# A decoder trunk with three attention branches: a new driver for the order of scores, outputs and projections

## The chip, the cores and the metric

The kernel runs on one core of a Trainium2 chip. The metric is the device time of one execution in microseconds (us), median of several runs.

## What is computed

One layer (sequence 2048, width 1024): a normalised input is projected once, and three causal token mixers of width 512 read their queries, keys, values and a gate path z from it. Their outputs, times SiLU of z, are projected, gated per channel by a sigmoid, summed and sent through the output projection. The inputs and outputs are float32.

```python
proj = rmsnorm(x, norm_g) @ w_in              # q, k, v, z of three branches, fox_f, merge gates
# differential: 4 heads of 2 score maps; ALiBi bias
pd = softmax(s[0]) - lam * softmax(s[1]);  oa = rmsnorm(pd @ v) 
# forgetting: 8 heads; bias c[q] - c[k], c the cumulative log_sigmoid of fox_f
ob = softmax(q @ k.T * scale + c_q - c_k) @ v
# dilated: 8 heads; windows of 128 steps at strides 1, 4 and 16, merged by their row maxima
y = stack([oa, ob, oc]) * silu(z)
merged = sum(sigmoid(merge_g) * (y @ w_branch), axis=branch)
out = rmsnorm(x + merged @ w_out, final_g)
```

## The kernel before

Every float32 operand is split into a high and a low float16 part, and a projection is three products (high by high, high by low, low by high) accumulated in one PSUM bank. After a start-up that normalises and transposes x and projects the first queries and keys, twelve groups are run (g 0 to 11): four differential, four forgetting and four dilated ones, each with the heads that fill 128 channels. A merge and an output projection close the kernel.

A group has two kinds of work on TensorE. The **fill** is projections: generators (`fill_v`, `proj_unit` of the next group, `fill_z`, `fill_gate`) in the queue of the class `Filler`, whose `step` runs the head of the queue for one step of six matmuls of 512 columns, counted at 216 ns each; `pump(ns)` runs steps until a credit of ns is used, and moves chains of side work (the finish of the group before, weight preparation) along. One projection of 128 channels over all tokens is TP = 4 x 24 x 216 ns = 20.736 us. The **attention** is written as jobs of 128 queries (two or four blocks in the dilated groups). A job has a generator S (scores) and a generator T (transposes):

- S: for each chunk of up to 512 keys two matmuls into one of three score banks (`scores`), then VectorE adds the bias and takes the row maximum into a float32 weight tile (L678, L1049; five such tiles, `E_SLOTS`). At the end ScalarE takes the exponential (L691, L1055); in the differential groups VectorE then combines the two maps (L784).
- T: ScalarE and VectorE split the weights into float16 parts in place (L702, L703), and SyncE issues a DMA transpose (L712) into one of three transposed tiles (`ET_SLOTS`). A generator for the output matmuls (`pv_mm`, L695 and L696) goes into the list `pvq`.

In the old `drive`, scores run up to three jobs ahead of the job that is transposed, as long as fewer than the allowed weight tiles are live; 0.2 of a job's share of the fill (`SFRAC`) is pumped between its chunks, the rest around its transposes and outputs. Outputs are run as soon as more than two (`LAG`) are in the list. The share of a job goes by a cost (differential: n(2 x 2 x 56 + 165) + 1500 for n key blocks), and the total is multiplied by 1.1 (`XF`).

What is written in this order is a priority. The framework's scheduler runs its own timing model over the program, and hands each engine, whenever the model has it free, the ready instruction that was written first. An instruction that is not ready in the model lets later ones pass; on the chip each engine then runs its list in order.

The functions that the diff touches, with the line numbers of the profile:

Of the kernel before, what the change touches and what calls it, by code (L numbers as in the profile page):

```python
# [19 lines left out]
P = 128  # L20
# [4 lines left out]
HD = 64  # L25
# [12 lines left out]

E_SLOTS = 5
V_SLOTS = 4  # L40
LAG = 2
SFRAC = 0.2
CHAIN = 1.3
XF = 1.1
XT = 1.1
PS = 1.5
WR = 1.0
W_SLOTS = 3
# [31 lines left out]
class Filler:  # L80
    def __init__(self):
        self.queue = []
        self.credit = 0.0
        self.chains = []
        self.wq = []
        self.wc = 0.0
# [18 lines left out]
    def step(self):  # L105
        while self.queue:
            c = next(self.queue[0], END)
            if c is END:
                self.queue.pop(0)
                continue  # L110
            return c
        return None

# [40 lines left out]
def tile_hybrid_trunk(  # L154
# [65 lines left out]
        V.tensor_mul(dst, dst, t)  # L220

    fl = Filler()
    sgx = ExitStack()
    xpool = sgx.enter_context(tc.tile_pool(name="xpool", bufs=1))
    xT = [[xpool.tile([P, KC, 512], F16, tag=f"xT{i}_{tg}", name=f"xT{i}_{tg}") for tg in range(4)] for i in range(2)]
# [142 lines left out]
    def mm_steps(dst, pairs, ns, per):  # L368
        n = len(pairs)
        for i, (l, r) in enumerate(pairs):  # L370
            T.matmul(dst, l, r, start=(i == 0), stop=(i == n - 1))  # L371
            if (i + 1) % per == 0 or i == n - 1:
                yield ns * per

    def mm_all(dst, pairs):
        n = len(pairs)
        for i, (l, r) in enumerate(pairs):
            T.matmul(dst, l, r, start=(i == 0), stop=(i == n - 1))

    def proj_unit(gr, j, tgs=range(4)):  # L380
        name = f"{gr['n']}_{j}"
# [258 lines left out]

    def scores(gr, u, q2s, qsl, ps, ksl):
        stk = gr["stk"][u]
        T.matmul(ps, stk[:, 0, qsl], stk[:, 1, ksl], start=True, stop=False)  # L643
        T.matmul(ps, q2s, stk[:, 1, ksl], start=False, stop=True)  # L644

    def make_q2(gr, u, i):
        stk = gr["stk"][u]
# [6 lines left out]
    def softmax_rows(gr, u, q2, qb, bias_of, diag, den_of, name):  # L654
        n = qb + 1
        nk = n * P
        nch = (n + 3) // 4
        qsl = slice(P * qb, P * qb + P)
        off = P * (qb % 4)
        pm = st1("pm", f"pm_{name}", 5)  # L660
        np_ = 0
        et = []
        for ch in range(nch):
            w = min(512, nk - 512 * ch)
            if ch % 2 == 0:
                et.append(e_tile(f"e_{name}_{ch // 2}", (P, 1280)))
                live[0] += 1
            ps = sc_bank(f"s_{name}_{ch}")
            scores(gr, u, q2[:, off:off + P], qsl, ps[:, :w], slice(512 * ch, 512 * ch + w))
            o = 256 + 512 * (ch % 2)  # L670
            segs = [(0, w, bias_of(512 * ch, w))]
            if diag is not None and ch == nch - 1:
                segs = [(w - P, P, diag)]
                if w > P:
                    segs.append((0, w - P, bias_of(512 * ch, w - P)))
            for a, sw, b in segs:
                with hp(H_TT):
# [3 lines left out]
            yield  # L681
# [12 lines left out]
    def pv_mm(po, eh, el, vv, first, last):  # L694
        T.matmul(po, eh, vv, start=first, stop=False)  # L695
        T.matmul(po[:, 0], el, vv[:, 0], start=False, stop=last)  # L696

    def split_in_place(t, c, w, scale):
        f = t[:, 256 + 512 * c:256 + 512 * c + w]
# [12 lines left out]
            Q.dma_start_transpose(eh[:, 0:2 * n // P], e[:, :n].bitcast(F16))  # L712
        return eh

    def transposed_pv(et, n, dd, vsel, scale, name, fin):
        box = {}

        def pv(i, eh):
            if i == 0:
                box["po"] = po_bank(f"po_{name}")  # L720
            po = box["po"][:, :2 * dd].rearrange("p (a c) -> p a c", a=2)
            for ch in range(2 * i, min(2 * i + 2, (n + 3) // 4)):
                nb = min(4, n - 4 * ch)
                for b in range(nb):
                    kb = 4 * ch + b
                    o = 8 * (ch % 2) + b
                    pv_mm(po, eh[:, o], eh[:, o + nb], vsel(kb), kb == 0, kb == n - 1)
# [21 lines left out]
    def jobs_diff(gr):  # L749
# [7 lines left out]
        def job(qb):  # L757
# [30 lines left out]
            def T_():  # L788
# [5 lines left out]
                yield from transposed_pv(hold["e"], n, P, lambda kb: gr["v"][kb // 4][:, kb % 4:kb % 4 + 5:4], lamA, name, fin)  # L794
# [128 lines left out]
    def jobs_fox(gr):  # L923
# [6 lines left out]
        def job(u, qb):  # L930
# [15 lines left out]
            def T_():  # L946
# [3 lines left out]
                def fin(po):  # L950
# [1 line left out]
                    A.activation(yq, po[:, 0], AF.Copy)  # L952
                    V.tensor_add(yq, yq, po[:, 1])

                yield from transposed_pv(hold["e"], n, HD, vsel, 2.0 ** 14, name, fin)

            ne = (n + 7) // 8
            nch = (n + 3) // 4
            return {"S": S_, "T": T_, "nS": nch, "nT": ne, "v": n,
                    "cost": n * (2 * 56 + 86)}  # L960

        return [job(u, qb) for u in range(2) for qb in range(NB)]

# [43 lines left out]
    def jobs_dil(gr):  # L1007
# [7 lines left out]
        def job(p, bs):  # L1015
# [11 lines left out]
            def S_():  # L1027
# [3 lines left out]
                for h in range(0, len(bs), 2):  # L1031
# [6 lines left out]
                    for a, b in enumerate(bs[h:h + 2]):  # L1038
# [17 lines left out]
                        yield  # L1056

            def T_():
                eh = transpose_tile(hold["e"], widths, 2.0 ** 14, name)

                def pv():
# [27 lines left out]
                            Q.dma_start(v, ro)  # L1089
                        yield  # L1090

                pvq.append(pv())
                yield

            return {"S": S_, "T": T_, "nS": len(bs), "nT": 1, "v": bs[-1] + 1 if p == 0 else NB,
                    "cost": sum(2 * kn[b] * (2 * 56 + 86) for b in bs)}

        return [job(p, list(range(b0, b0 + (2, 2, 4)[p]))) for p in range(3) for b0 in range(0, NB, (2, 2, 4)[p])]

# [75 lines left out]

    pvq = []

    def drive(gr, cap, limit, total_fill):
        jobs = jobmakers[gr["br"]](gr)
        n = len(jobs)  # L1180
        wts = [jb["cost"] + 1500 for jb in jobs]
        tw = sum(wts)
        sj = 0
        sgen = jobs[0]["S"]()
        for i, jb in enumerate(jobs):
            share = total_fill * wts[i] / tw
            tgen = jb["T"]()
            while True:
                while sj < n and (sj <= i or sj - i <= limit) and live[0] < cap:
                    if next(sgen, END) is not END:  # L1190
                        fl.pump(SFRAC * total_fill * wts[sj] / tw / jobs[sj]["nS"])
                    else:
                        sj += 1
                        if sj < n:
                            sgen = jobs[sj]["S"]()
                        else:
                            gr["Sdone"] = True
                assert sj > i
                while gr["vdone"] < jb["v"]:
                    c = fl.step()  # L1200
                    assert c is not None and c >= 0, (gr["n"], i)
                if next(tgen, END) is END:
                    break
                sh = (1 - SFRAC) * share / jb["nT"]
                while len(pvq) > LAG:
                    for _ in pvq.pop(0):
                        fl.pump(0.5 * sh)
                        sh *= 0.5
                fl.pump(sh)
# [250 lines left out]
    T.transpose(pb[:, :KC], g8, ident[:KC, :KC])  # L1460
    V.tensor_copy(gx, pb[:, :KC])
    gm = st.tile([P, 1], F32, tag="gm", name="gm")
    V.tensor_reduce(gm, gx, axis=AX.X, op=ALU.max, apply_absolute_value=True)
# [31 lines left out]
        w_start()  # L1495

    TP = 4 * 24 * 216
    for g in range(12):
        gr = groups[g]
        nx = groups[g + 1] if g < 11 else None  # L1500
        total = (2 + NG[g]) * TP
        fl.add(fill_v(gr))
        if g > 0:
            gr["post"] = fl.chain(post(groups[g - 1]))
        if nx is not None:
            fl.add(proj_unit(nx, 0))
            fl.add(fill_z(gr))
            total += TP
            if g == 2:
                fprep = fl.chain(prep_f())  # L1510
                fl.add(fill_f())
                total += 20000
# [4 lines left out]
        else:  # L1517
            fl.add(fill_gate((22,)))
            fl.add(tail_fill(gr))
            total = 4 * TP * XT  # L1520
# [89 lines left out]
```

## Time and profile before

| what | value |
|---|---|
| median of 3 runs | 2789.35 us (2782.4 to 2799.62) |
| profiled execution, first to last instruction | 2783.2 us |
| TensorE busy in it | 2624.6 us |
| VectorE busy | 2088.2 us |
| ScalarE busy | 1661.3 us |
| GpSimd busy | 376.8 us |

The profile is of one execution. Its own time is given as the span from its first to its last instruction; it lies 6 us below the median of the runs and inside their range. Busy shares are sums over the span and say nothing on which engine another one waits for.

### The profile page before, as it was taken

To read this page: it belongs to the slowest core of one execution; us is meant where nothing else is said; L and a number is where in the kernel's file an instruction comes from. 1 tells how busy PE (TensorE), PEld (TensorE's weight loads), DVE (VectorE), ACT (ScalarE), POOL (GpSimd) and SP (SyncE) were. 2 spreads that over 40 slices of the span, in tenths; PEclk is the share of its full clock that TensorE was granted. 3 is DMA by queue.
4 is the path that set the end of the run, shared out by engine and by line. 5 is a ranking of instruction groups with operands and counts; after the bars stand their busy time and mean duration, and the time that the engine had idled before them with its cause. 6 is when DMAs were issued, how large, how long until landed. Compare 5 with 4: busy or idle time off the path is not lost.

```text
span 2783.2 us, 47508 instructions
## 1 busy us (share of the span) xinstructions
PE 2624.6 (94%) x16216; PEld 1376.9 (49%) x16216; DVE 2088.2 (75%) x7048; ACT 1661.3 (60%) x3616; POOL 376.8 (14%) x529
## 2 busy tenths in 40 slices
PE   7999899999999999999899999999999999999998
PEld 4454445455444454444444444554554545444565
DVE  8687877978877878768778776658568575778955
ACT  6466666656556676666666665656657678535411
POOL 0000200200201112002102110005033051210000
PEclk9999999989999999999999999999999999999999
DMA  4345444445454786787787777648568599875232
GB/s 160 76 84 114 74 100 107 104 76 123 87 100 106 135 173 142 155 154 157 144 155 145 141 144 156 132 108 180 126 132 185 125 210 230 226 210 163 80 121 76
DMA packets 979268, 376.94 MB, mean 135 GB/s; under 512 B 834120, under 2 KB 939344, under 8 KB 977488
## 3 DMA queue, kind: packets, MB, share of 16 engines
q1 hardware_dynamic: 979024, 373.90, 61.9%
q8 instruction: 127, 2.08, 0.3%
q14 instruction: 117, 0.96, 0.1%
HBM read 118.14 MB, written 59.05 MB: 64 GB/s over the span
## 4 chain that ended last, share of the span: by engine, by line
PE 52%; DVE 19%; DMA 17%; ACT 7%; issue 4%; POOL 1%; SPq 1%; DVEq 0%; ACTq 0%; POOLq 0%
DMA eT_g<-e_g 11%; PE pg L371 10%; PE pbr L371 8%; PE pq_g L371 8%; PE pz_g L371 5%; PE pout L1417 4%; PE s_g L643 4%; DVE e_g L678 4%; PE s_g L644 4%; DVE e_g L703 4%; PE po_g L695 3%; ACT e_g L691 3%; PE pv_g L371 2%; PE pout L1418 2%; DMA w_g<-in_w_in_dram 2%
## 5 line engine op out<-in xcount | busy, mean ns | idle before, releaser
L371 PE MATMUL pg<-xT,w_g 128*128 128x512 f16 x2304 | 554.5, 382 | 0.3 <-ACT xT L638 0.3
L691 ACT ACTIVATE e_g<-e_g,nm_g,c_g 128x1024 f32<-128x1024 f32 (+7 forms) x384 | 377.6, 984 | 263.5 <-DVE nm_g L685 227.9
L643 PE MATMUL s_g<-stk_g 128*128 128x512 f16 (+3 forms) x1024 | 352.6, 352 | 50.2 <-DVE pm_g L678 45.6
L703 DVE SCALAR_TENSOR_TENSOR e_g<-e_g 128x512 f16<-128x512 f32 (+2 forms) x480 | 316.0, 670 | 80.9 <-ACT e_g L702 79.6
L371 PE MATMUL pq_g<-xT,w_q 128*128 128x512 f16 x1536 | 369.5, 387 | 5.0 <-DVE stk_g L398 4.4
L695 PE MATMUL po_g<-v_g,eT_g 128*128 128x128 f16 (+1 forms) x2232 | 306.7, 235 | 61.5 <-DMA eT_g<-e_g 56.2
L644 PE MATMUL s_g<-stk_g,q_g 128*128 128x512 f16 (+3 forms) x1024 | 351.9, 354 | 2.6 <-DMA q_g<-stk_g 2.6
L371 PEld LDWEIGHTS <-w_g 128*128 128x128 f16 x2304 | 218.9, 99 | 229.9 <-issue 5.3
L702 ACT ACTIVATE e_g<-e_g 128x512 f16<-128x512 f32 (+2 forms) x480 | 265.0, 569 | 104.4 <-DVE e_g L703 102.3
L696 PE MATMUL po_g<-v_g,eT_g 128*128 128x64 f16 (+1 forms) x2232 | 286.3, 201 | 0.0
L695 PEld LDWEIGHTS <-eT_g 128*128 128x128 f16 x2232 | 207.2, 99 | 141.7 <-DMA eT_g<-e_g 88.4
L371 PE MATMUL pz_g<-xT,w_z 128*128 128x512 f16 x1152 | 273.1, 380 | 2.5 <-DVE stk_g L398 2.4
L371 PE MATMUL pv_g<-xT,w_v 128*128 128x512 f16 x1152 | 270.3, 382 | 4.3 <-DVE vs_g L527 4.3
L1055 ACT ACTIVATE e_g<-e_g,nm_g,c_g 128x256 f32<-128x256 f32 (+1 forms) x384 | 207.8, 543 | 91.4 <-DVE nm_g L1051 90.3
L371 PE MATMUL pbr<-u,w_b 128*128 128x512 f16 x1152 | 253.5, 381 | 0.0
L678 DVE CUSTOM_DVE_ANT_0 e_g<-s_g,bias_g 128x512 f32<-128x512 f32 (+3 forms) x320 | 187.8, 605 | 59.7 <-DMA eT_g<-e_g 51.6
L696 PEld LDWEIGHTS <-eT_g 128*128 128x128 f16 x2232 | 204.5, 99 | 49.5 <-issue 5.5
L371 PEld LDWEIGHTS <-w_q 128*128 128x128 f16 x1536 | 146.5, 100 | 166.4 <-issue 13.4
L678 DVE CUSTOM_DVE_ANT_0 e_g<-s_g,R_g 128x512 f32<-128x512 f32 (+3 forms) x288 | 171.2, 596 | 62.9 <-DMA eT_g<-e_g 55.4
L1049 DVE CUSTOM_DVE_ANT_0 e_g<-s_g,bd_g 128x256 f32<-128x256 f32 (+1 forms) x384 | 122.8, 361 | 89.0 <-PE s_g L644 44.7
L371 PEld LDWEIGHTS <-w_b 128*128 128x128 f16 x1152 | 112.9, 98 | 133.5 <-issue 2.2
L644 PEld LDWEIGHTS <-q_g 128*128 128x128 f16 x1024 | 109.2, 107 | 140.6 <-issue 62.3
(471 smaller groups left out, 4174.3 us busy)
## 6 DMA issues: line engine op xcount, KB each, us to landing
gd<-gs SPq DMA_DIRECT2D x96, 256.0 KB, 2.7
gt<-gd SPq DMA_DIRECT2D x24, 1024.0 KB, 5.3
w_g<-in_w_in_dram SPq DMA_DIRECT2D x24, 512.0 KB, 4.4
ud<-y_g SPq DMA_DIRECT2D x48, 256.0 KB, 2.8
od_g<-ro_g SPq DMA_DIRECT2D x64, 132.0 KB, 1.9
xb<-in_x_dram SPq DMA_DIRECT2D x16, 512.0 KB, 5.8
q_g<-stk_g SPq DMA_DIRECT2D x128, 64.0 KB, 2.2
w_q<-in_w_in_dram SPq DMA_DIRECT2D x32, 256.0 KB, 4.1
```

The source lines that it names most:

```text
L371: T.matmul(dst, l, r, start=(i == 0), stop=(i == n - 1))
L643: T.matmul(ps, stk[:, 0, qsl], stk[:, 1, ksl], start=True, stop=False)
L644: T.matmul(ps, q2s, stk[:, 1, ksl], start=False, stop=True)
L678: V.tensor_tensor_reduce(out=et[ch // 2][:, o + a:o + a + sw], in0=ps[:, a:a + sw], in1=b, scale=1.0, scalar=-3e38, op0=ALU.add, op1=ALU.m ...
L691: A.activation(e[:, 256:256 + w], e[:, 256:256 + w], AF.Exp, bias=nm, scale=gr["c"][u], accum_out=den_of(i))
L695: T.matmul(po, eh, vv, start=first, stop=False)
L696: T.matmul(po[:, 0], el, vv[:, 0], start=False, stop=last)
L702: A.activation(h[:, :w], f, AF.Copy, scale=scale)
L703: V.scalar_tensor_tensor(h[:, w:], f, scale, h[:, :w], op0=ALU.mult, op1=ALU.subtract)
L1049: V.tensor_tensor_reduce(out=e[:, o + w * u:o + w * u + w], in0=ps[:, 256 * u:256 * u + w], in1=bt[p, u][:, 256 - w:256], scale=1.0, scala ...
L1055: A.activation(eu, eu, AF.Exp, bias=nm[:, 2 * a + u:2 * a + u + 1], scale=gr["c"][u], accum_out=sm[:, a, 2 + u:3 + u])
L1417: T.matmul(po, ah, wo[un][k], start=k == 0, stop=False)
```

## The change

`drive` is rewritten. Jobs are written strictly one after the other, scores and then transposes, with no run-ahead. After each chunk of w key columns the loop pumps total_fill x w / (sum of w), where w is the chunk's columns (twice two blocks in the dilated groups) plus `STEP` = 150. The factors `SFRAC`, `XF`, `XT` and `LAG` are gone, and the dilated groups pump 8 us of fill (`lead`) ahead of their first chunk.

The `Filler` gets a clock that counts what TensorE is given: each fill step by its count, each chunk by 0.84 w, each output step by 600. An output generator is entered with the time clock + `LAT` (12000 for differential, 9000 for the other groups) and is run when the clock has passed it, between fill steps too, or earlier when three are waiting and a new transpose is to be written (`pv_room`). After the last job, `drain` pumps what is left in steps of 1300 with the outputs between.

Each score and output matmul also gets a dependence in order alone (no semaphore) on the last fill matmul written before it, so that the scheduler may not move it ahead of that. It may still move fill ahead of a score or an output that is not ready. These ties hold in the twelve groups alone.

```diff
-LAG = 2
-SFRAC = 0.2
-XF = 1.1
-XT = 1.1
+LAT = (12000, 9000, 9000)
+STEP = 150
...
+            if c:
+                self.clock += max(c, 0)
             return c
...
+    def after_fill(ins):
+        if pe_last[0] is not None:
+            tc.add_manual_dep(ins.ins, pe_last[0], mybir.DependencyInfo(mybir.DependencyClass.NoSync, mybir.DependencyReason.DATA),
+                              reason="order")
+
+    def mm_fill(*a, **k):
+        ins = T.matmul(*a, **k)
+        if pe_last[0] is not None:
+            pe_last[0] = ins.ins.name
+
+    def mm(*a, **k):
+        after_fill(T.matmul(*a, **k))
...
-            T.matmul(dst, l, r, start=(i == 0), stop=(i == n - 1))
+            mm_fill(dst, l, r, start=(i == 0), stop=(i == n - 1))
...
-        T.matmul(ps, stk[:, 0, qsl], stk[:, 1, ksl], start=True, stop=False)
-        T.matmul(ps, q2s, stk[:, 1, ksl], start=False, stop=True)
+        mm(ps, stk[:, 0, qsl], stk[:, 1, ksl], start=True, stop=False)
+        mm(ps, q2s, stk[:, 1, ksl], start=False, stop=True)
...
+            pv_room()
             eh = transpose_tile(e, [512] * (w // 512) + ([w % 512] if w % 512 else []), scale, f"{name}_{i}")
-            pvq.append(pv(i, eh))
+            pv_add(pv(i, eh), gr, n)
...
-            return {"S": S_, "T": T_, "nS": 2 * nch, "nT": ne, "v": n, "cost": n * (2 * 2 * 56 + 165)}
+            return {"S": S_, "T": T_, "w": 2 * (nk + STEP * nch)}
...
+    def pv_add(gen, gr, need):
+        pvq.append((gen, fl.clock + LAT[gr["br"]], gr, need))
+
+    def pv_run():
+        gen, _, gr, need = pvq.pop(0)
+        while gr["vdone"] < need:
+            c = fl.step()
+            assert c is not None and c >= 0, gr["n"]
+        for _ in gen:
+            fl.clock += 600
+
+    def pv_room():
+        while len(pvq) >= ET_SLOTS:
+            pv_run()
+
+    def pv_due():
+        while pvq and fl.clock >= pvq[0][1]:
+            pv_run()
+
+    def pump(ns):
+        fl.pump_chains(ns * CHAIN)
+        fl.credit += ns
+        while fl.credit > 0:
+            c = fl.step()
+            if c is None or c < 0:
+                fl.credit = 0.0
+                return
+            fl.credit -= c
+            pv_due()
+
+    def drive(gr, total_fill, lead):
         jobs = jobmakers[gr["br"]](gr)
+        tw = sum(jb["w"] for jb in jobs)
+        total_fill -= lead
+        pump(lead)
+        for jb in jobs:
+            for w in jb["S"]():
+                fl.clock += 0.84 * w
+                pv_due()
+                pump(total_fill * w / tw)
+            run_all(jb["T"]())
+        gr["Sdone"] = True
+
+    def drain():
+        while fl.queue:
+            pump(1300)
         while pvq:
-            run_all(pvq.pop(0))
+            pv_run()
+        fl.drain()
...
-        total = (2 + NG[g]) * TP
+        total = (2 + NG[g]) * TP + (TP if nx is not None else 0)
...
-        drive(gr, E_SLOTS - (2 if gr["br"] == 2 else 0), 3, total * XF)
-        fl.drain()
+        drive(gr, total, 8000 if gr["br"] == 2 else 0)
+        drain()
+    pe_last[0] = None
```

## Rows read from the trace of the kernel before

**Rows 1.** The page, part 1: busy us of each engine, share, instructions.
```profile
PE 2624.6 (94%) x16216; PEld 1376.9 (49%) x16216; DVE 2088.2 (75%) x7048; ACT 1661.3 (60%) x3616; POOL 376.8 (14%) x529
```

**Rows 2.** Busy time by stretch: length, five engines, clock, DMA share, GB/s.
```profile
130.00:960.00 830.00, 784.00 (x4766) 407.59 (x4765) 673.86 (x2174) 509.89 (x1020) 89.19 (x89) 0.98 0.49 101
960.00:1680.00 720.00, 666.17 (x4736) 348.51 (x4735) 547.02 (x1910) 468.96 (x953) 104.86 (x163) 1.00 0.77 149
1680.00:2400.00 720.00, 691.89 (x4198) 368.82 (x4196) 493.99 (x1855) 477.50 (x1268) 146.05 (x222) 0.97 0.75 162
2400.00:2784.00 384.00, 373.87 (x1990) 194.78 (x1988) 277.81 (x744) 129.97 (x230) 31.95 (x45) 0.99 0.46 140
```

**Rows 3.** Timeline of TensorE, forgetting stage: start us, us, instructions of one kind merged.
```profile
1059.80 0.38 PE L644 MATMUL s_g<-stk_g,q_g 128*128 128x512 f16 x1
1060.02 4.48 PE L371 MATMUL pq_g<-xT,w_q 128*128 128x512 f16 x20
```

**Rows 4.** Waits of TensorE, 130 to 960 us: total us, times, longest.
```profile
PE s_g L643 <- DVE pm_g L678: 27.9, 44, 3.9
PE po_g L695 <- DMA eT_g<-e_g: 7.1, 11, 2.4
PE pv_g L371 <- DVE vs_g L527: 4.3, 4, 2.2
```

**Rows 5.** Waits of TensorE, 960 to 1680 us.
```profile
PE po_g L695 <- DMA eT_g<-e_g: 37.4, 33, 2.3
PE s_g L643 <- DVE pm_g L678: 11.8, 16, 1.5
```

**Rows 6.** Waits of TensorE, 1680 to 2400 us.
```profile
PE po_g L695 <- DMA eT_g<-e_g: 11.6, 11, 3.1
PE pq_g L371 <- DVE stk_g L398: 3.9, 2, 2.1
```

**Rows 7.** Timeline of TensorE, a dilated group of stride 16.
```profile
2350.33 0.43 PE L644 MATMUL s_g<-stk_g,q_g 128*128 128x128 f16 x1
2350.57 0.42 PE L643 MATMUL s_g<-stk_g 128*128 128x128 f16 x1
```

**Rows 8.** The weight tiles e: steps with least, median and greatest duration in ns.
```profile
L702 ACT ACTIVATE e_g<-e_g x480: 292/617/634, 883.5 to 2371.3; 128x512 f16<-128x512 f32 x125, 128x256 f16<-128x256 f32 x13, 128x128 f16<-128x128 f32 x11, 128x384 f16<-128x384 f32 x11
L703 DVE SCALAR_TENSOR_TENSOR e_g<-e_g x480: 277/684/1778, 885.0 to 2373.7; 128x512 f16<-128x512 f32 x125, 128x256 f16<-128x256 f32 x13, 128x128 f16<-128x128 f32 x11, 128x384 f16<-128x384 f32 x11
...
L691 ACT ACTIVATE e_g<-e_g,nm_g,c_g x384: 477/1073/1244, 99.3 to 1659.1; 128x1024 f32<-128x1024 f32 x132, 128x128 f32<-128x128 f32 x12, 128x384 f32<-128x384 f32 x12, 128x640 f32<-128x640 f32 x12
...
L712 SPq DMA_TRANSPOSE eT_g<-e_g x368: 1167/1812/6631, 105.8 to 2376.1; - x184
L678 DVE CUSTOM_DVE_ANT_0 e_g<-s_g,bias_g x320: 269/683/693, 98.3 to 867.9; 128x512 f32<-128x512 f32 x136, 128x128 f32<-128x128 f32 x8, 128x256 f32<-128x256 f32 x8, 128x384 f32<-128x384 f32 x8
L678 DVE CUSTOM_DVE_ANT_0 e_g<-s_g,R_g x288: 278/680/693, 882.3 to 1654.3; 128x512 f32<-128x512 f32 x112, 128x128 f32<-128x128 f32 x16, 128x384 f32<-128x384 f32 x16
```

**Rows 9.** Timeline of TensorE in a long differential job.
```profile
447.91 2.75 PE L371 MATMUL pg<-xT,w_g 128*128 128x512 f16 x12
450.50 0.33 PE L643 MATMUL s_g<-stk_g 128*128 128x384 f16 x1
450.82 1.46 PE L371 MATMUL pg<-xT,w_g 128*128 128x512 f16 x6
```

**Rows 10.** Waits of VectorE, one row from each stage, in order of the stages.
```profile
DVE e_g L678 <- DMA eT_g<-e_g: 52.4, 31, 3.9
...
DVE e_g L678 <- DMA eT_g<-e_g: 70.7, 43, 4.8
...
DVE e_g L1049 <- DMA eT_g<-e_g: 30.4, 20, 3.9
```

**Rows 11.** DMA issues, 960 to 1680 us: count, median us from issue to landing.
```profile
eT_g<-e_g SPq DMA_TRANSPOSE x176, 4.3
```

**Rows 12.** Busy time and clock around the forget gate's matmuls.
```profile
595.00:615.00 20.00, 20.00 (x193) 12.02 (x192) 15.73 (x51) 10.44 (x22) 0.50 (x2) 0.83 0.27 58
```

More of the change, by code (lines that the diff above doesn't have):

```diff
@@ L83, in __init__ @@
         self.credit = 0.0
+        self.clock = 0.0
         self.chains = []
@@ L222, in tile_hybrid_trunk @@
     fl = Filler()
+    pe_last = [None]
+    def after_fill(ins):
[8 more added lines that the diff above has]
+        after_fill(T.matmul(*a, **k))
     sgx = ExitStack()
@@ L377, in mm_all @@
         for i, (l, r) in enumerate(pairs):
-            T.matmul(dst, l, r, start=(i == 0), stop=(i == n - 1))
+            mm_fill(dst, l, r, start=(i == 0), stop=(i == n - 1))
     def proj_unit(gr, j, tgs=range(4)):
@@ L680, in softmax_rows @@
                 np_ += 1
-            yield
+            yield w + STEP
         nm = st1("nm", f"nm_{name}")
@@ L694, in pv_mm @@
     def pv_mm(po, eh, el, vv, first, last):
-        T.matmul(po, eh, vv, start=first, stop=False)
-        T.matmul(po[:, 0], el, vv[:, 0], start=False, stop=last)
+        mm(po, eh, vv, start=first, stop=False)
+        mm(po[:, 0], el, vv[:, 0], start=False, stop=last)
     def split_in_place(t, c, w, scale):
@@ L713, in transpose_tile, with transposed_pv @@
         return eh
-    def transposed_pv(et, n, dd, vsel, scale, name, fin):
+    def transposed_pv(gr, et, n, dd, vsel, scale, name, fin):
         box = {}
@@ L792, in fin @@
                     A.activation(o_tile(f"ot_{name}"), y[:, qb], AF.Square, accum_out=ssq[:, qb:qb + 1])
-                yield from transposed_pv(hold["e"], n, P, lambda kb: gr["v"][kb // 4][:, kb % 4:kb % 4 + 5:4], lamA, name, fin)
+                yield from transposed_pv(gr, hold["e"], n, P, lambda kb: gr["v"][kb // 4][:, kb % 4:kb % 4 + 5:4], lamA, name, fin)
             ne = (n + 7) // 8
             nch = (n + 3) // 4
-            return {"S": S_, "T": T_, "nS": 2 * nch, "nT": ne, "v": n, "cost": n * (2 * 2 * 56 + 165)}
+            return {"S": S_, "T": T_, "w": 2 * (nk + STEP * nch)}
         return [job(qb) for qb in range(NB)]
@@ L953, in fin @@
                     V.tensor_add(yq, yq, po[:, 1])
-                yield from transposed_pv(hold["e"], n, HD, vsel, 2.0 ** 14, name, fin)
+                yield from transposed_pv(gr, hold["e"], n, HD, vsel, 2.0 ** 14, name, fin)
             ne = (n + 7) // 8
             nch = (n + 3) // 4
-            return {"S": S_, "T": T_, "nS": nch, "nT": ne, "v": n,
-                    "cost": n * (2 * 56 + 86)}
+            return {"S": S_, "T": T_, "w": n * P + STEP * nch}
         return [job(u, qb) for u in range(2) for qb in range(NB)]
@@ L1055, in S_ @@
                                 A.activation(eu, eu, AF.Exp, bias=nm[:, 2 * a + u:2 * a + u + 1], scale=gr["c"][u], accum_out=sm[:, a, 2 + u:3 + u])
-                        yield
+                        yield 2 * w + STEP
             def T_():
+                pv_room()
                 eh = transpose_tile(hold["e"], widths, 2.0 ** 14, name)
@@ L1090, in pv @@
                         yield
-                pvq.append(pv())
+                pv_add(pv(), gr, NB if p else bs[-1] + 1)
                 yield
-            return {"S": S_, "T": T_, "nS": len(bs), "nT": 1, "v": bs[-1] + 1 if p == 0 else NB,
-                    "cost": sum(2 * kn[b] * (2 * 56 + 86) for b in bs)}
+            return {"S": S_, "T": T_, "w": sum(2 * P * kn[b] + STEP for b in bs)}
         return [job(p, list(range(b0, b0 + (2, 2, 4)[p]))) for p in range(3) for b0 in range(0, NB, (2, 2, 4)[p])]
@@ L1176, in tile_hybrid_trunk @@
     pvq = []
-    def drive(gr, cap, limit, total_fill):
-        jobs = jobmakers[gr["br"]](gr)
[L1180 to L1209, printed above, removed]
@@ L1459, in tile_hybrid_trunk @@
     pb = ps_tr.tile([P, 512], F32, tag="tr", name="pb_g")
-    T.transpose(pb[:, :KC], g8, ident[:KC, :KC])
+    T_first = T.transpose(pb[:, :KC], g8, ident[:KC, :KC])
     V.tensor_copy(gx, pb[:, :KC])
@@ L1497, in tile_hybrid_trunk @@
     TP = 4 * 24 * 216
+    pe_last[0] = T_first.ins.name
     for g in range(12):
@@ L1507, in tile_hybrid_trunk @@
             fl.add(fill_z(gr))
-            total += TP
             if g == 2:
@@ L1511, in tile_hybrid_trunk @@
                 fl.add(fill_f())
-                total += 20000
+                total += 12000
             fl.add(fill_gate(range(G0[g], G0[g + 1])))
@@ L1519, in tile_hybrid_trunk @@
             fl.add(tail_fill(gr))
-            total = 4 * TP * XT
         fl.credit = 0.0
-        drive(gr, E_SLOTS - (2 if gr["br"] == 2 else 0), 3, total * XF)
-        fl.drain()
+        drive(gr, total, 8000 if gr["br"] == 2 else 0)
+        drain()
+    pe_last[0] = None
     oc = []
```

## The prediction

> **What bounds the kernel now.** I read four views in this order: the busy shares and clock of the page, the busy time by stage, who ended TensorE's waits in each stage, and the durations of the steps behind those waits. The page gives TensorE 2624.6 us of work in 2783.2 us, the most of any engine, VectorE 2088.2 us [rows 1]. The differential, forgetting and dilated groups fill three stretches (130 to 960, 960 to 1680, 1680 to 2400 us); the projections ahead of them and the merge and output behind them stay as they are, and in 2400 to 2784 us TensorE is busy 373.87 of 384 us [rows 2]. So the change can act on 2270 us.
>
> There TensorE shows 46, 53.8 and 28.1 us without work, together 128 us [rows 2]. That is too little, because a matmul's record runs on past the start of its successor: 20 fill matmuls of 512 columns in a row take 4.48 us, and one alone is shown as 0.38 us, so they follow each other every (4.48 - 0.38)/19 = 0.216 us and each record is 0.163 us longer than its share [rows 3]. Every stop is therefore 0.163 us longer than shown. Two waits carry most of it. The first score matmul of a chunk (L643) waits for VectorE to empty a score bank: 27.9 us in 44 waits in the differential stage, 11.8 us in 16 in the forgetting stage [rows 4, 5]. The first output matmul (L695) waits for the DMA transpose of the weights: 7.1 us in 11, 37.4 in 33, 11.6 in 11 [rows 4 to 6]. The clock adds to this: its granted mean is 0.98, 1.00 and 0.97 in the three stages, that is 0.02 x 830 + 0.03 x 720 = 38 us of full-speed work lost at the half level [rows 2].
>
> One loss that looks alike is not a stop: in the dilated groups score matmuls of 128 columns follow each other every 0.24 us although nothing is waited for, against 0.216 us for 512 columns elsewhere [rows 3, 7]. Those read strided tokens, and no order changes that.
>
> The Trainium skill (TensorE: Matmul & The Clock Gate, Back-to-back issue gap) gives about 131 ns as the sustained spacing of 512-column matmuls; by it the 8064 projection and merge matmuls (72 projections of 96, and 1152) would have 85 ns each to give, an estimate of 685 us, and TensorE would not be the bound. The trace differs, with 216 ns [rows 3], and the measurement decides.
>
> **Spreading the scores.** Before, only 0.2 of a job's fill is put between its chunks. The largest differential job has weight 16 x 389 + 1500 = 7724 of 76904 and 8 chunks, so its share of 1.1 x 5 x 20.736 us is 11.5 us, and 0.29 us stands between chunks in the written order. With two score matmuls (0.43 us) that is 0.72 us a chunk, less than the 0.683 us of VectorE's reduction of that chunk and all else on that engine [rows 8], which is busy for 0.81 of the stage (673.86 of 830) [rows 2]. After, a chunk of 512 weighs 662 of 46816, so 1.47 us of fill stands behind it and 1.9 us pass per chunk. Three score banks then cover some 5.7 us of VectorE's delay in place of 2.2 us.
>
> The gain is not the whole of it, because the scheduler already moves ready fill ahead of a score that its model holds back: around 450 us, 12 fill matmuls run, then two score matmuls, then 6 fill matmuls [rows 9]. What is left are the places where VectorE was later than the model. The stops on scores are 39.7 us shown in 60 waits, with 60 x 0.163 = 9.8 us hidden: 49.5 us. Bounds: all goes (-49.5), or nothing goes as the written order was already corrected (0). I take two thirds, **-33 us**, nearer the full end, since bank depth in time more than doubles and since jobs no longer run ahead. VectorE now stands 52.4, 70.7 and 30.4 us at a reduction that waits for a weight-tile slot held by an unfinished transpose [rows 10]: the old loop lets scores run up to three jobs ahead until all five slots are live, so that its next reduction meets a slot just being emptied. In the new order a job's transposes are written before the next job's scores; a forgetting job of 16 blocks holds two slots, and three are free. Of differential jobs (four slots) only one is free, so there the wait may stay.
>
> **Outputs a fixed time behind.** The output step is put 12 us (differential) or 9 us of counted TensorE time behind the writing of its transpose. Is that late enough? For the first tile of a long forgetting job the steps after the last score are: reduction 0.680, exponential 1.073, split 0.617 and 2 x 0.684, landing of the transpose 4.3 us [rows 8, 11]: 8.0 us if no engine makes it wait, and about two more for the second tile, which is exponentiated and split behind it. With VectorE 0.76 busy in that stage (547.02 of 720) [rows 2] there is queueing on top. So the due time falls at or before the landing, and the scheduler's model, not the fixed time, still places many output steps. That is the same footing as before. The stops today are 56.1 us shown in 55 waits, with 9 us hidden: 65 us, or 1.18 us each. Bounds: all goes (-65), or every tile of every stage fares as the forgetting ones do, (37.4 + 33 x 0.163)/176 = 0.24 us a tile, for 368 tiles [rows 5, 8, 11] 89 us, +24. I take **-15 us**: near the middle, leaning to a gain because VectorE's splits are held up less.
>
> **Ties.** A score or output matmul may no longer move ahead of the last fill matmul written before it. When fill waits for a bank, scores and outputs behind it on TensorE now wait too, and with them VectorE's reductions and ScalarE's exponentials. Such stops on fill are seldom now: 4.3 us on pv in the differential stage, 3.9 us on pq in the dilated one [rows 4, 6]. Bounds 0 to +8 (each costs double); I take **+4 us**.
>
> **Clock.** The half level comes where TensorE had stopped or ran very small matmuls; 595 to 615 us, where the 384 matmuls of the forget gate run, has 0.83 [rows 12] and stays. Fewer stops give back some: bounds -30 to 0, **-12 us**, about a third of 38.
>
> **Edits at nothing.** The fill of a group is the same work, dealt out at a pace of 1.0 in place of 1.1; the last projection of the next group still runs behind the last score, and now has output steps between its matmuls, which covers the end of a job's chain. The 8 us of fill ahead of the first dilated score is fill taken from later. DMA issues keep their number; weight loads, gate stores and transposes all stand on SyncE's one queue, in an order that moves with the scores. If that cover were gone, a group end would cost one chain of some 8 to 10 us; eleven of them are the +100 us at most that I count to the slower rival.
>
> **Sum.** -33 - 15 - 12 + 4 = -56 us on the profiled execution, 2783.2 - 56 = 2727 us. Its span lies 6 us under the median of the runs (2789.35), so 2733 us is to be compared with that. Ends: -49.5 - 65 - 30 = -144 gives 2645; +24 + 8 = +32 gives 2821.
>
> **Rivals.** *The slots are the limit, no change: about 2785 us.* Buffers stay as they are: five weight tiles, three transposed ones, three score banks. If the stops come from slots, the same waits appear elsewhere. For it: the 153 us that VectorE spends on slots [rows 10], and the already spread order [rows 9]. Against it: the old loop fills the slots by its own rule. The Trainium skill (Perfetto Trace Analysis, Identifying the Most-Contended Engine) says that the same gap repeating on the engine that should be saturated can mean too little SBUF or PSUM for the next tile; this rule speaks for this rival, and rows 10 agree in part.
>
> *The change does not do what it says, also about 2785 us.* Ties hold scores behind fill, but nothing holds fill behind scores, so the scheduler may deal out nearly the old order. I count it with the first.
>
> *Slower: outputs are due too early.* If jobs written one after the other leave less time between score and output than the old run-ahead did, output steps stop TensorE in the two stages where they mostly do not today. At 1.18 us a stop and half of 368 tiles this is 184 x 1.18 = 217, less the 65 of today, +152, with nothing gained elsewhere: 2941 us. It decides from some 35 more stops than the 55 of today, that is about 90 of 368, because those eat the 33 + 12 - 4 = 41 us gained.
>
> **How the numbers follow.** One per cent, 28 us, is about what a measurement of this kernel can tell from no change. Forecast, faster by more than that (below 2761): 0.6. The two rivals without change: 0.2. Slower (above 2817): 0.2. The range 2645 to 2821 takes in both ends of the unknown costs; it leaves out most of the slower rival and a few in a hundred below.
>
> **What would show it.** Right: in 130 to 1680 us the waits of L643 on the bank fall to a third, those of VectorE on weight-tile slots fall in the forgetting stage, and output waits fall a little or stay. The clock of the first and third stage rises by about 0.01. Wrong: more than 90 output stops, or a stage that grows while fill stands still for a bank; then the due times or the ties cost more than spreading gives. If every wait keeps its size at other places, the slots were the limit.

## The result and the profile after

The changed kernel takes 2818.38 us against 2790.14 us of the kernel before (medians of 4 runs each): a ratio of 1.0101, 95% interval 1.0077 to 1.0125. It is slower by one per cent, where 2733 us, faster by two per cent, was forecast.

The page of the changed kernel, part 1, answers to [rows 1]: each engine does nearly the same work.

```profile
PE 2624.3 (93%) x16216; PEld 1378.6 (49%) x16216; DVE 2090.8 (74%) x7048; ACT 1671.8 (59%) x3617; POOL 370.3 (13%) x529
```

Busy time by stretch, in the columns of [rows 2] (the last stretch is cut at 2820 us here):

```profile
130.00:960.00 830.00, 763.50 (x4609) 395.96 (x4607) 660.75 (x2114) 497.21 (x988) 91.59 (x87) 0.98 0.47 96
960.00:1680.00 720.00, 665.70 (x4681) 348.46 (x4678) 544.98 (x1912) 466.52 (x947) 91.55 (x157) 0.99 0.76 148
1680.00:2400.00 720.00, 682.22 (x4226) 367.06 (x4227) 482.42 (x1832) 487.87 (x1275) 148.46 (x224) 0.98 0.75 158
2400.00:2820.00 420.00, 403.78 (x2158) 209.19 (x2156) 306.90 (x832) 146.44 (x261) 33.89 (x50) 0.99 0.48 144
```

In 130 to 960 us TensorE is now busy for 763.5 us in place of 784.0; the clock of the third stretch gained 0.01, that of the second lost as much. The first value matmuls of the groups tell where the 34.5 us of span came from (time from that of one stage to that of the next, read off both timelines): differential groups 782.0 to 796.7, forgetting ones 789.0 to 803.5, dilated ones 709.3 to 710.8, what follows the last output 395.5 to 402.3, the start 3 us less. The third differential group alone went from 201.2 to 221.9 us; the second and the fourth became shorter.

Waits of TensorE in the three stretches, which answer to [rows 4 to 6] (L237 is the helper through which both scores and outputs are now issued, so the tile tells them apart):

```profile
PE s_g L237 <- DVE pm_g L694: 34.1, 30, 2.9
PE po_g L237 <- DMA eT_g<-e_g: 22.2, 23, 2.5
...
PE po_g L237 <- DMA eT_g<-e_g: 42.7, 42, 3.3
PE s_g L237 <- DVE pm_g L694: 9.3, 12, 2.2
...
PE po_g L237 <- DMA eT_g<-e_g: 21.6, 16, 3.3
```

And VectorE at a weight tile that an unfinished transpose still holds, stage by stage, as in [rows 10]:

```profile
DVE e_g L694 <- DMA eT_g<-e_g: 77.9, 34, 5.2
...
DVE e_g L694 <- DMA eT_g<-e_g: 69.1, 48, 3.5
...
DVE e_g L1065 <- DMA eT_g<-e_g: 14.2, 12, 3.0
```

Output stops tripled in the differential stage (7.1 us to 22.2), grew in the forgetting stage (37.4 to 42.7) and nearly doubled in the dilated one (11.6 to 21.6). Score stops in the differential stage are fewer and longer (27.9 us in 44 to 34.1 in 30). VectorE's wait for tiles grew where only one slot is free (52.4 to 77.9); in the forgetting stage it stayed (70.7 to 69.1), where it was to fall; in the dilated one it fell (30.4 to 14.2).

How late an output comes can be read tile by tile, from the issue of its transpose to its first output matmul (the 368 transposes and outputs of a trace paired in order; each wait of an output on a transpose falls on such a first matmul). The median was 8.1, 5.8 and 10.9 us in the differential, forgetting and dilated groups before the change, and is 4.8, 5.2 and 7.5 us after it. The transpose lands 4.1 to 4.5 us after its issue (medians by stage) in both kernels. So the outputs moved nearer to the landing in every stage.

### The profile page after: what moved, and what is told of

The parts are those of the page before. It is cut to its first block, busy times and chain, and to the rows that moved or that the text cites. A ratio compares the mean times of both kernels' runs of the same rounds, so it can differ in the third digit from the quotient of the medians.

```text
span 2817.7 us, 47534 instructions
## 1 busy us (share of the span) xinstructions
PE 2624.3 (93%) x16216; PEld 1378.6 (49%) x16216; DVE 2090.8 (74%) x7048; ACT 1671.8 (59%) x3617; POOL 370.3 (13%) x529
## 4 chain that ended last, share of the span: by engine, by line
PE 45%; DVE 22%; DMA 19%; ACT 6%; issue 5%; POOL 2%; SPq 1%; DVEq 0%; POOLq 0%; ACTq 0%
DMA eT_g<-e_g 12%; PE pg L232 10%; PE s_g L237 7%; PE pbr L232 6%; PE pq_g L232 6%; DVE e_g L694 5%; PE pz_g L232 5%; DVE e_g L719 4%; PE pout L1448 4%; PE po_g L237 3%; ACT e_g L707 2%; PE pout L1449 2%; PE pv_g L232 2%; DMA w_g<-in_w_in_dram 1%; DVE e_g L801 1%
## 5 line engine op out<-in xcount | busy, mean ns | idle before, releaser
L237 PE MATMUL s_g<-stk_g 128*128 128x512 f16 (+3 forms) x1024 | 354.4, 352 | 47.2 <-DVE pm_g L694 43.8
L237 PE MATMUL po_g<-v_g,eT_g 128*128 128x128 f16 (+1 forms) x4464 | 291.3, 219 | 95.9 <-DMA eT_g<-e_g 86.4
L237 PE MATMUL s_g<-stk_g,q_g 128*128 128x512 f16 (+3 forms) x1024 | 356.3, 354 | 1.3 <-DMA q_g<-stk_g 1.3
L232 PEld LDWEIGHTS <-w_g 128*128 128x128 f16 x2304 | 227.1, 99 | 254.2 <-issue 7.7
L237 PEld LDWEIGHTS <-eT_g 128*128 128x128 f16 x4464 | 251.8, 99 | 182.1 <-DMA eT_g<-e_g 131.6
L232 PE MATMUL pv_g<-xT,w_v 128*128 128x512 f16 x1152 | 276.2, 383 | 9.7 <-ACT w_v L318 5.2
L232 PEld LDWEIGHTS <-w_v 128*128 128x128 f16 x1152 | 111.7, 99 | 133.2 <-issue 7.3
L237 PEld LDWEIGHTS <-q_g 128*128 128x128 f16 x1024 | 109.8, 107 | 133.8 <-issue 56.7
L232 PEld LDWEIGHTS <-w_z 128*128 128x128 f16 x1152 | 112.7, 99 | 125.4 <-issue 1.4
```

Source lines behind the costliest of these rows:

```text
L232: ins = T.matmul(*a, **k)
L237: after_fill(T.matmul(*a, **k))
```

## Experiments

For a comparison across runs I read the same two waits in one window, 100 to 2420 us. The kernel before, then the changed one:

```profile
PE po_g L695 <- DMA eT_g<-e_g: 56.2, 55, 3.1
PE s_g L643 <- DVE pm_g L678: 45.6, 64, 3.9
```

```profile
PE po_g L237 <- DMA eT_g<-e_g: 86.4, 81, 3.3
PE s_g L237 <- DVE pm_g L694: 43.8, 43, 2.9
```

With 0.163 us hidden in each stop, outputs cost 56.2 + 55 x 0.163 = 65 us before and 86.4 + 81 x 0.163 = 100 us after, scores 56 and 51 us: +34 and -5, together 29 of the 34.5 us of span. The table has these two waits for each run, and the run's time beside the kernel before on the same chip.

| run | median us | ratio (95% interval) | outputs: us, stops | scores: us, stops |
|---|---|---|---|---|
| before | 2790.14 | | 56.2, 55 | 45.6, 64 |
| changed | 2818.38 | 1.0101 (1.0077 to 1.0125) | 86.4, 81 | 43.8, 43 |
| e1_no_ties | 2820.21 | 1.0110 (1.0092 to 1.0128) | 87.8, 81 | 40.6, 42 |
| e2_ties_old_driver | 2827.27 | 1.0136 (1.0121 to 1.0151) | 62.6, 62 | 47.4, 63 |
| e3_outputs_later | 2826.13 | 1.0128 (1.0113 to 1.0143) | 78.2, 70 | 39.0, 43 |
| e4_gate_credit | 2832.86 | 1.0151 (1.0134 to 1.0168) | 99.9, 87 | 37.6, 41 |
| f1_old_no_run_ahead | 2862.64 | 1.0254 (1.0235 to 1.0273) | 93.4, 90 | 38.3, 35 |
| f2_old_even_pace | 2828.45 | 1.0128 (1.0111 to 1.0145) | 56.1, 54 | 62.8, 70 |
| f3_old_pace_1 | 2833.56 | 1.0151 (1.0133 to 1.0170) | 64.4, 65 | 52.8, 67 |
| f5_new_run_ahead | 2831.82 | 1.0145 (1.0125 to 1.0164) | 57.6, 59 | 63.1, 78 |
| n1_old_sfrac_022 | 2807.96 | 1.0056 (1.0041 to 1.0071) | 59.8, 65 | 50.7, 71 |
| n2_old_pace_109 | 2840.73 | 1.0176 (1.0159 to 1.0192) | 56.3, 58 | 70.1, 87 |
| n6_old_sfrac_018 | 2823.92 | 1.0098 (1.0072 to 1.0125) | 57.7, 49 | 53.3, 68 |
| n7_old_pace_111 | 2811.97 | 1.0058 (1.0038 to 1.0079) | 68.1, 63 | 42.8, 58 |
| n3_new_step_160 | 2828.14 | 1.0128 (1.0106 to 1.0150) | 90.6, 83 | 43.2, 42 |
| n4_new_due_300_later | 2825.10 | 1.0119 (1.0104 to 1.0134) | 95.9, 83 | 44.0, 44 |
| n5_new_step_140 | 2828.35 | 1.0126 (1.0097 to 1.0155) | 94.8, 85 | 42.6, 45 |
| n8_old_chain_132 | 2790.32 | 0.9999 (0.9987 to 1.0012) | 54.8, 53 | 45.9, 63 |
| s7_new_four_slots | 2819.30 | 1.0092 (1.0065 to 1.0120) | 87.0, 86 | 36.4, 43 |
| s8_new_four_slots_held | 2946.71 | 1.0553 (1.0535 to 1.0571) | 124.3, 84 | 73.8, 62 |

My first theory was the rival of the prediction: outputs are due too early, and so they stop TensorE. Its rivals were the ties, and a count of work that does not exist in the third differential group.

**The ties.** The new driver without them (below: the line that starts them is gone), and the old one with them.

```diff
-    pe_last[0] = T_first.ins.name
```

> The changed kernel without its ties in order: scores and outputs may again move ahead of fill. If the ties make the loss (scores and outputs held behind a stalled fill), the time falls from 2818 to some 2795 and output stops from 86 us to some 60. If outputs are written too early (they are due before their transpose has landed), the order hardly changes, because nothing is ready to move ahead, and the time stays at 2810 to 2825.

> The old driver with the ties alone. If the ties make the loss, 2805 to 2820. If the loss is the new writing order (output times, no run-ahead), the old driver is as before within 0.5%: 2780 to 2800.

Without ties the changed kernel takes the same time, 2820 us with the same 81 output stops, though 28% of the places in TensorE's list hold another kind of matmul. On the old driver the time rose by 37 us with hardly any more stops on outputs or scores (fill that waits for a bank in `pq` grew from 5.2 to 17.9 us). The two runs did not agree with one cost of the ties, and that was the first sign that something else moves the time. A cost of the ties smaller than what the nudges below move is not shown by either.

**Outputs later.**

```diff
-LAT = (12000, 9000, 9000)
+LAT = (24000, 18000, 18000)
```

> The changed kernel with outputs due 24 us (differential) and 18 us (others) behind, in place of 12 and 9; at most three still wait. If outputs are due too early, output stops fall from 86 us to 50 or less and the time to 2775 to 2795. If the loss lies in the scores written without run-ahead, output stops fall but scores wait more, and the time stays within 10 us of 2818. If the three transposed tiles are the limit, SyncE waits for outputs again (72 us in the kernel before, none listed in the changed one) and the time is 2800 to 2820.

Output stops fell only from 81 to 70, and the time rose to 2826 us. By stage the run says more. In the dilated groups the outputs did come later (10.9 us behind the issue of their transpose, 7.5 in the changed kernel), and there TensorE's stops on them went from 21.6 us in 16 to one (the row below), and the stage from 710.8 to 685.1 us; 12 us of that came back behind the last output (the stage's time alone proves little: e1's takes 684.4 us with its stops in place, and 19 us more behind it). In the two other stages the later due times hardly reached the chip: 5.4 us in place of 4.8, and 5.2 as before. In the forgetting groups `pv_room` is the reason. Counted while the driver writes the program, 176 of their 192 outputs are written because three are waiting, at 10.4 us of the driver's clock (median) and not at 18; in the changed kernel it is 76 of 192. In the differential groups it is 57 of 96, and why the others come no later stays open. The forgetting stage grew by 16 us all the same.

```profile
PE po_g L237 <- DMA eT_g<-e_g: 2.1, 1, 2.1
```

So the theory does not fall: where the outputs moved, their stops went away, and in the two first stages it was hardly tested, in the forgetting one because three transposed tiles keep the outputs early. SyncE's waits for outputs need not show that limit, since the driver writes an output ahead of the fourth transpose: they are 28 us here and 72 in the kernel before (and 32 in the changed one, for which the expectation has none).

**The forget gate's counts.**

```diff
-            if c:
+            if c and c not in (4000, 5000):
                 self.clock += max(c, 0)
...
-                total += 12000
+                total += 20000
```

> The changed kernel with the forget gate's pauses (4000 and 5000 ns in which no matmul runs) left out of the clock that sets output times, and its fill counted as 20 us again in place of 12. If the third differential group's 20.7 us of loss comes from these counts, that group falls by 10 us or more and the kernel to some 2805. If it comes from waits on VectorE and weight tiles as elsewhere, the time stays within 5 us of 2818.

The third group still takes 218.7 us (first value matmuls at 485.5 and 704.2 us; 221.9 in the changed kernel), and other groups grew; the time is 2833 us, above either expectation. The counts are not the cause.

**One part alone on the old driver.** No run-ahead, spreading, and the pace of the fill:

```diff
-        drive(gr, E_SLOTS - (2 if gr["br"] == 2 else 0), 3, total * XF)
+        drive(gr, E_SLOTS - (2 if gr["br"] == 2 else 0), 0, total * XF)
```

> The old driver with one part of the change alone: scores may not run ahead of the job that is transposed. If the lost run-ahead makes the loss (a job's chain from scores to landed transpose is then not covered), 2810 to 2830, with output stops above 80 us. If not, 2785 to 2800.

```diff
-SFRAC = 0.2
+SFRAC = 0.9
```

> The old driver with another part alone: 0.9 of a job's fill between its chunks in place of 0.2. If even spreading is good in itself, as the prediction had it, score stops fall from 65 us to 40 and the time to some 2770. If scores written in a burst are what gives the chain its start, 2810 to 2830.

```diff
-XF = 1.1
-XT = 1.1
+XF = 1.0
+XT = 1.0
```

> The old driver with the fill's factors at 1.0 in place of 1.1. If the slower pace (fill and side chains finished later) makes the loss, 2805 to 2825, and the part behind the last output grows by the 7 us seen in the changed kernel. If not, 2785 to 2800.

And run-ahead put back on the new driver:

```diff
...
-            run_all(jb["T"]())
+                while late and (live[0] >= cap or len(late) > 2):
+                    run_all(late.pop(0)["T"]())
+            late.append(jb)
+            while late and live[0] >= cap:
+                run_all(late.pop(0)["T"]())
...
```

> The changed kernel with run-ahead: a job's transposes are written only when the weight tiles are all live or two more jobs are scored. If the lost run-ahead makes the loss, 2780 to 2800. If it is the output times or the scatter of any new order, 2810 to 2835.

TensorE's two waits in f1 (old driver, no run-ahead), then f2 (old driver, even pace), then f5 (new driver with run-ahead):

```profile
PE po_g L695 <- DMA eT_g<-e_g: 93.4, 90, 4.4
PE s_g L643 <- DVE pm_g L678: 38.3, 35, 2.9
```

```profile
PE s_g L643 <- DVE pm_g L678: 62.8, 70, 3.3
PE po_g L695 <- DMA eT_g<-e_g: 56.1, 54, 3.3
```

```profile
PE s_g L237 <- DVE pm_g L694: 63.1, 78, 2.8
PE po_g L237 <- DMA eT_g<-e_g: 57.6, 59, 3.9
```

Here the two kinds of stop come apart. Without run-ahead (the changed kernel, e1, e3, e4, f1 and the nudges of the new driver) the table has 70 to 90 output stops and 35 to 45 score stops; with run-ahead (the kernel before, e2, f2, f3, f5 and the nudges of the old driver) 49 to 65 and 58 to 87. Taking run-ahead from the old driver turns 55 output stops into 90, giving it to the new one turns 81 into 59, and score stops go the other way each time. Spreading does not lower score stops: f2 has more of them than the kernel before. f2 puts 0.9 x 11.5 / 8 = 1.3 us of fill behind a chunk, near the 1.47 us of the changed kernel. But no part given back brings the time back. All three parts alone cost 34 to 68 us, more than the whole change, and f1 and f3 (like e2 above) took longer than either of their expectations allowed.

Nor do the two waits carry all of the time. f1 is 77 us longer than the kernel before in the profiled execution: TensorE stands still 52 us longer, and its busy time for the same 16216 matmuls is 24 us longer (2649.0 against 2624.6), at a granted clock of 0.976 in place of 0.985 over the span.

**Nudges.** If every change costs something, is the kernel before only one good draw? Four changes of the old driver that were meant to be too small to matter (`SFRAC` 0.22 and 0.18, `XF` 1.09 and 1.11), and three of the new one (`STEP` 160 and 140, due times 0.3 us later):

> A nudge of the old driver: 0.22 of a job's fill between its chunks in place of 0.2. If the time of the kernel before is what its way of ordering gives, 2780 to 2800. If it is one good draw among many orders (each change of an order, however small, makes another list for each engine), 2805 to 2835, as the larger changes gave.

> A second nudge of the old driver: the fill's factor 1.09 in place of 1.1. As for the first: 2780 to 2800 if the old way of ordering gives the time, 2805 to 2835 if it was a good draw.

> A nudge of the new driver: each chunk weighs 160 beside its columns in place of 150. If the time of the changed kernel is what its way gives, 2810 to 2826; if it is a draw, another one anywhere in 2785 to 2840, with the gains and losses in other groups than before.

> A second nudge of the new driver: outputs due 0.3 us later. 2810 to 2826 if the way of ordering gives the time; 2785 to 2840 if it is a draw. A later due time by itself is worth at most 112 output stops x 0.3 = 30 us, if it only shortened them.

> A third nudge of the new driver: 140 beside a chunk's columns in place of 150. The nudges so far gave 2825 and 2828 beside 2818; if the new way scatters as little as that, 2810 to 2835.

> A third nudge of the old driver: 0.18 of a job's fill between its chunks. If the kernel before is a good draw among orders of a mean near 2825, 2800 to 2845; if its value is the middle of its neighbours, 2775 to 2800.

> A fourth nudge of the old driver: the fill's factor 1.11. As for the third: 2800 to 2845 if the kernel before is a good draw, 2775 to 2800 if not.

The old driver's neighbours take 2808, 2841, 2824 and 2812 us, mean 2821 (2815 with the kernel before among them); the new one's 2828, 2825 and 2828, with the changed kernel itself mean 2825. So a factor of 1.09 in place of 1.1 costs 49 us, more than the whole change, with 23 more score stops than the kernel before. (The 112 output stops in the expectation of n4 are 81 in the table's window.) In all four nudges of the old driver about half of the loss or more lies outside the two waits. n6 has 9 us more in them than the kernel before and is 41 us longer: TensorE stands still 30 us longer in all and is busy 11 us longer (2635.8 us, at a granted clock of 0.982).

A last nudge of the old driver (`CHAIN` 1.32 in place of 1.3, side chains alone) tells what a nudge does:

> A fifth nudge of the old driver, one that changes neither scores nor fill: side chains move 1.32 times as fast as the fill in place of 1.3. 2800 to 2845 if the kernel before is a good draw among orders, as the four other nudges say; 2780 to 2798 if only nudges of the score and fill pace cost something.

It is 2790 us, and its matmuls stand in the same order from first to last as in the kernel before (by the tiles they write, all 16216). So do the working instructions of VectorE, ScalarE and GpSimd. It is thus no neighbour but the kernel before once more, and shows how well a time repeats. In the four other nudges 65 to 76% of the places hold the same kind of matmul. My expectation was that any neighbour is slower; what holds is narrower: where the lists stay, the time stays.

**Weight tiles.** One of five held unused through the differential and forgetting groups of the new driver, in a first try by a tile that is written ahead of them and read behind them:

```diff
+        if g == 0:
+            hold_t = e_tile("hold")
+            V.memset(hold_t[:, :1], 0.0)
+        if g == 8:
+            V.tensor_copy(st1("hr", "hold_r"), hold_t[:, :1])
```

> The changed kernel with one of the five weight tiles held unused through the eight differential and forgetting groups. If weight-tile slots set the stops, VectorE's waits on unfinished transposes (167 us) grow by half or more and the two stages by 60 us or more: 2880 and above. If slots have slack, 2810 to 2840. The third differential group, in which the forget gate takes such a tile for a while, should then lose its excess over its neighbours (some 28 us), since they now have no more than it.

The time is that of the changed kernel, but so is everything: the scheduler moved the reading copy up at once, as nothing held it back, and the tile was free at 67 us. The one instruction that reads it, in the view of that tile (the one that fills it stands at 65.6 us):

```profile
L1537 DVE COPY hold_r<-hold x1: 142/142/142, 67.2 to 67.2; 128x1 f32<-128x1 f32 x1
```

The run tells nothing on tiles. It has the changed kernel's order of matmuls, and its time within 1 us. The second try makes the copy read a scale of the first dilated group:

```diff
...
+            V.tensor_copy(hold_t[:, :1], groups[8]["cst"][:, 0, 0:1])
```

> As the run before it, but the held weight tile is now freed by a copy of a scale of the first dilated group, which exists only near the end of the forgetting groups; in the run before it the tile was freed at 67 us, so that run was the changed kernel again. If weight-tile slots set the stops, VectorE's waits on unfinished transposes grow by half or more and the two stages by 60 us or more: 2880 and above. If slots have slack, 2810 to 2840.

The tile is held until 1591 us, through the four differential groups and three of the four forgetting ones; the last begins at 1606.7 us. The view of that tile, VectorE's wait for tiles in 100 to 2420 us (the changed kernel, then this run), and the differential stage from its first value matmul to that of the next stage, with the clock third from the end (again the changed kernel, then this run):

```profile
L1537 DVE COPY hold<-c_g x1: 144/144/144, 1591.5 to 1591.5; 128x1 f32<-128x1 f32 x1
```

```profile
DVE e_g L694 <- DMA eT_g<-e_g: 148.4, 83, 5.2
DVE e_g L694 <- DMA eT_g<-e_g: 252.8, 127, 5.2
```

```profile
104.00:901.00 797.00, 738.36 (x4413) 381.89 (x4414) 630.47 (x2034) 473.19 (x943) 70.39 (x61) 0.98 0.46 94
104.00:991.00 887.00, 770.62 (x4412) 389.85 (x4413) 634.06 (x2030) 472.57 (x941) 72.18 (x61) 0.93 0.41 84
```

The kernel takes 2947 us, 128 more. The differential stage, where a job holds four tiles, grew from 796.7 to 887.4 us, far more than any order moved it (782 to 816 us in all other runs). So there the number of weight tiles sets the stops. Of these 91 us TensorE stands still some 58 us longer; the other 32 us are chiefly the same work at a lower clock, 0.93 in place of 0.98. For the forgetting stage nothing is shown: it grew from 803.5 to 826.2 us, but 14 of these 23 us lie in its last group, which has the tile back, and the dilated groups grew by 17 us too. More than five do not fit beside the other tiles, so a sixth wasn't tried.

The third group's excess does not go: it takes 244.7 us beside 215.7 and 226.3 (first value matmuls at 304.7, 520.4, 765.1 and 991.4 us). The expectation of s7 was wrong there. The gate's tile comes from the same five (`e_tile("ft")`, in use here from 673 to 694 us), so that group has three tiles for a while where its neighbours have four, and neither run tells whether that tile is what it loses by.

## Why the prediction was wrong

The forecast was 2733 us and 2818 us was measured. That lies inside the range only at its slow end (2821), and by luck: outputs passed their bound by 10 us, and the other terms came out near nothing. The sign that was to tell the slower outcome, more than 90 output stops, did not come either (81): the gains that these stops were to eat were not there.

**What bounds the kernel** held: TensorE's work is the same 2624 us, and the difference is mostly stops on scores and outputs, +34 - 5 us shown and hidden, of 34.5.

**Spreading the scores (-33 us)** failed, in its size (-5 in 100 to 2420 us; in the rows of the prediction 49.5 us became 34.1 + 9.3 + 42 x 0.163 = 50.2, where they were to fall to a third) and in its reason. The sum took the 1.9 us between chunks as what relieves the banks. f2 has nearly that spacing on the old driver and 62.8 us of score stops in place of 45.6. What lowers their number is that jobs no longer run ahead: f1 has the old spacing, and 35 stops. That VectorE's waits for tiles would fall in the forgetting stage failed too (70.7 to 69.1 us).

**Outputs (-15 us, bounds -65 to +24)** failed in sign: +34 us, outside its bounds. The argument that outputs are due at or before the landing was right, but the step "the same footing as before" was not: in the old order a job's scores ran up to three jobs ahead of the outputs, so the chain behind the scores had its time; written job after job it does not. The outputs moved from 8.1, 5.8 and 10.9 us behind the issue of their transpose to 4.8, 5.2 and 7.5 us. f1 and f5 show this from both sides: without run-ahead the old driver has 5.1, 5.1 and 7.4 us, with it the new one has 5.5, 5.1 and 12.4. The rival built on it, outputs too early, had the right mechanism and the wrong size (2941 us). Later due times took the stops away in the dilated groups (e3); in the two other stages they hardly made the outputs later, so whether they would help there stays open. Nor does the run's time follow these stops: with run-ahead f5 has 22 fewer of them than the changed kernel and takes 2832 us.

**Clock (-12 us):** the granted mean is 0.98, 0.99 and 0.98 against 0.98, 1.00 and 0.97 [rows 2], no gain. **Ties (+4 us):** no cost to be seen on the new driver (e1).

**The step under all of them failed too.** I took the stops of the kernel before as what its way of ordering gives, and subtracted from them. They are those of one list of instructions. Orders next to it, by the same way, take 2808 to 2841 us; the new way's neighbours lie at 2825 to 2828. Between the two ways no difference can be told: their means are 4 us apart, or 10 with the kernel before counted in, and the old one's neighbours spread by 33. What the change lost is the particular order of the kernel before. But from the neighbours' mean of 2821 us, too, the 56 us to be gained are not there, so the terms failed as well as the base. The nudges of the new driver moved its order less (92 to 99% of the places are the same), so its spread is less well known than the old one's.

**The slots rival** was half right: the number of tiles sets the stops of the differential stage (s8), but that did not mean no change. The rule that I set beside it (the Trainium skill, Perfetto Trace Analysis, Optimization Strategy under Identifying Performance Opportunities: the same gap repeating on the engine that should be saturated can mean too little memory for the next tile) agrees with s8, where one tile fewer costs that stage 91 us.

What stays open: what in the kernel before's order saves its 31 us over its neighbours, and whether a sixth weight tile would free both ways. That the order decides is inferred: the nudges change nothing but the order of writing (and with it, which buffer a tile gets), and n8 and s7, which keep TensorE's list, keep the time. Why this order is better is not shown. Nor is it known how 0.2 and 1.1 were chosen: if they were picked by timing, the lead over the neighbours is what picking leaves, and no accident. None of the 18 runs beats the kernel before.

## What to carry to other kernels

When a scheduler deals out the order from a model, measure the neighbours of the kernel before (one factor, one per cent) ahead of crediting a rewrite or blaming it: here that spread, 33 us, is larger than the change. Stops on scores and on outputs are exchanged by run-ahead, so cost them together. Read an experiment's own quantity before its time: e3 was to make outputs later, and in two of three stages it hardly did. The buffers between the two, five weight tiles, are worth more than either order where a job holds four: one tile fewer cost the differential stage 91 us.

## What I had not expected

The same 16216 matmuls, with five weight tiles, take from 2790 to 2863 us by the order in which the instructions are written, 2.5% apart, while the medians of the same order agree within 0.1% (n8: 0.9999, interval 0.9987 to 1.0012). A copy that is only written late does not hold a tile: it ran 1.6 us after the tile was filled (s7).
